# A hybrid SSM and sparse-attention model on one core: the SSM's scan in four chunks of 64 tokens instead of two of 128

## The chip, the core and the metric

The kernel runs on one core of a Trainium2 chip. Its engines work side by side, each through its own queue in order: TensorE (PE; PEld are its weight loads), VectorE (DVE), ScalarE (ACT), GpSimd (POOL) and SyncE (SP), which here only issues DMAs. The metric is the device time of one execution in microseconds. The kernel before takes 858.65 us (median of 3 runs, 856.76 to 860.2).

## The reference: what is computed

Two layers on 256 tokens of width 1024, all in float32. Each layer adds a mixer and then a gated feed-forward block of width 2816. The mixer runs a state-space branch (SSM) and an attention branch with three kinds of keys, and merges them by gates. The SSM is what the change touches:

```python
def s5_mixer(u, a_re, a_im, log_dt, b_re, b_im, c_re, c_im, d, w_glu):
    ...
    mag = jnp.exp(lr * dt)
    ab_re = mag * jnp.cos(li * dt)
    ab_im = mag * jnp.sin(li * dt)
    ...
    bu_re = jnp.einsum('bsgh,gph->bsgp', uf, b_re.astype(f32))
    ...
    _, _, x_re, x_im = lax.associative_scan(complex_affine_combine, (a_seq_re, a_seq_im, bb_re, bb_im), axis=1)
    y = (jnp.einsum('bsgp,ghp->bsgh', x_re, c_re.astype(f32))
         - jnp.einsum('bsgp,ghp->bsgh', x_im, c_im.astype(f32))
         + d.astype(f32).reshape(SSM_GROUPS, SSM_GROUP) * uf)
```

So each of 32 x 64 states follows x[t] = a x[t-1] + b[t] with one complex a of its own over the 256 tokens.

## The kernel before, in words

States lie on the 128 partitions in 16 slices a layer, which are worked on in 4 groups q of 4 slices; tokens run along the columns. A complex scan is made real by rotation: the input is multiplied by a table of cos and sin of the angle times t, scanned with the real magnitude, and turned back. The tables (E, one for cos and one for sin) hold 16 slices times TC = 128 steps; they start again in each chunk of 128 tokens, so two chunks make 256 tokens.

- `rot_powers` squares the rotation again and again: pw[i] is its power 2^i, and pw[7], times the magnitude's power, carries the state over a whole chunk. `rot_half` doubles the table in 7 steps from 1 to 128 columns, for one half (8 slices) at a time, three VectorE operations a step (two into E, one into tb). Layer 0 builds its tables at the beginning of its mixer (`p_par`, `p_tb`), layer 1's are asked for in layer 0's feed-forward.
- `ssm_a(q, h)` ("A" in ORDER) takes a group's input through small matmuls into psb, multiplies it with the tables (bc, bs, 512 columns each) and combines into z, laid out as chunk, part, slice, step. POOL writes the magnitudes into rm.
- `ssm_b2(q)` ("B") scans chunk 0: two scans (real and imaginary part) of 4 x 128 = 512 columns. Then four operations on POOL (cy three times, then z) rotate the last state of the chunk and add it to the first column of chunk 1. `ssm_c2(q)` ("C") scans chunk 1.
- `ssm_d(q, h)` ("D") multiplies z with the tables (pr) and sums over the states by matmuls into psy, then adds the direct term (yf), applies gelu and splits (y).

Other work in the same stretch: the projections' rope (`rope2`: a copy by ScalarE, four small DMAs into the one buffer tagged sw, three operations rt, sw, rt on VectorE; in layer 1 the sw product runs on POOL), the compression of keys (`c_in`: DMAs of kvc into kr, which has the same one buffer, sums kk on VectorE; `c_w1`: matmuls ps_c), the gates' matmuls ps_g, and the splits of weights into two float32r parts (wh by ScalarE, wl by VectorE). rb is the norm's scale for each token: VectorE computes it as dg, TensorE spreads it (ps_n), ScalarE copies it.

The instructions of all engines are put in order by a planner that runs a timeline of its own while the kernel is built: of what is ready on an engine in that timeline it takes what stands first in the program, which is the list ORDER. So an item may run well before or after its neighbours in ORDER, and the queues' order changes when sizes change. The pad tiles only set addresses.

Of the kernel before, what the change touches and what calls it, by code (L numbers as in the profile page):

```python
# [4 lines left out]
F32 = mybir.dt.float32  # L5
# [9 lines left out]
T = 256  # L15
KD = 8
NF = 22
NS = 16
TC = 128
NCMP = 15  # L20
CH = 1024
NEG = -1e30
# [17 lines left out]
for _name, _w in [("ropec", 256), ("ropes", 256), ("ident", 128), ("causal", 128),  # L40
# [48 lines left out]
def body(tc, ctx, d, out):  # L89
# [5 lines left out]
    raws = pool("raws", NRAW)  # L95

    pad = lambda name, n: pool(name).tile([128, n // 4], F32, name=name)
    pad("pad0", 96)
    whs = pool("whs", NWH)
    pad("pad3", 128)  # L100
    wls = pool("wls", NWL)
# [96 lines left out]
    N2 = L * NS  # L198
    par = cst.tile([128, 5, N2], F32, name="par")
    pi = cst.tile([128, N2], I32, name="pi")  # L200
    pw = cst.tile([128, 8, 3, N2], F32, name="pw")
    R, WR, WI, FR, FI = range(5)
    def tt(o, a, b, op, e=V):
        return e.tensor_tensor(o, a, b, op=op)  # L204
# [82 lines left out]
    def rot_powers():  # L287

        t = cst.tile([128, N2], F32, name="tpw")
        V.tensor_copy(pw[:, 0, 0], par[:, WR])  # L290
        ts(pw[:, 0, 1], par[:, WI], -1.0, OP.mult)
        V.tensor_copy(pw[:, 0, 2], par[:, WI])
        for i in range(7):
            stt(t, pw[:, i, 2], -2.0, pw[:, i, 2], OP.mult, OP.mult)
            stt(pw[:, i + 1, 1:3], pw[:, i, 1:3], 2.0, pw[:, i, 0:1].to_broadcast([128, 2, N2]), OP.mult, OP.mult)
            ts(pw[:, i + 1, 0], t, 1.0, OP.add)
        tt(pw[:, 7], pw[:, 7], par[:, R:R + 1].to_broadcast([128, 3, N2]), OP.mult)

    def rot_room(e):
        E = pp.tile([128, 2, NS, TC], F32, name="E", tag="E")  # L300
# [1 line left out]
        e.memset(E[:, 1, :, 0:1], 0.0)  # L302
        return E

    def rot_half(E, l, h, e, tpool, nsb=2, steps=range(7)):

        NQ = 8
        j = slice(h * NQ, (h + 1) * NQ)
        jl = slice(l * NS + h * NQ, l * NS + (h + 1) * NQ)
        tb = tpool.tile([128, 2, NQ, TC // 2], F32, name="tb", tag="sb", bufs=nsb)  # L310
        for i in steps:
            s = 1 << i
            br = pw[:, i, 0:1, jl, None].to_broadcast([128, 2, NQ, s])
# [96 lines left out]
    def mixer(l, nm, sc, first, mp, sm_):  # L410
# [132 lines left out]
        def ssm_a(q, h):  # L543

            B = sv["B"]
            Ec, Es = sv["sc"][:, 0], sv["sc"][:, 1]
            if h == 0:
                rt = mp.tile([128, 4, TC], F32, name="rm", tag="rm", bufs=1)
                G.tensor_copy(rt, par[:, R, sl0 + 4 * q:sl0 + 4 * q + 4, None].to_broadcast([128, 4, TC]))
                G.memset(rt[:, :, 0:1], 0.0)  # L550
                st[q] = mp.tile([128, 2, 2, 4, TC], F32, name="z", tag="z", bufs=NZ), rt
            z = st[q][0]
            psb = [bank("psb", "aux") for _ in range(2)]
            with row():
                for c in range(2):
                    for a in range(2):
                        r = slice(64 * h + 32 * a, 64 * h + 32 * a + 32)
                        PE.matmul(psb[a][:, c * T:(c + 1) * T], B[r, q, c, :], uy[q][r, :], start=True, stop=True,
                                  skip_group_check=True)
            bc = mp.tile([128, 2, 2, 2, TC], F32, name="bc", tag="sb", bufs=2)  # L560
            bs = mp.tile([128, 2, 2, 2, TC], F32, name="bs", tag="sb", bufs=2)
            for a in range(2):
                j = 4 * q + 2 * h + a
                src = psb[a].rearrange("p (r t) -> p r t", t=TC)
                for o, e in ((bc, Ec), (bs, Es)):
                    tt(o[:, a].rearrange("p r c t -> p (r c) t"), src,
                       e[:, j, None, :].to_broadcast([128, 4, TC]), OP.mult)
# [10 lines left out]

        def ssm_b2(q):

            z, rt = st[q]
            scan(q, 0)
            cy = sm_.tile([128, 2, 2, 4], F32, name="cy", tag="cy", bufs=2)
            zl = z[:, 0, :, :, TC - 1]
            e = eng("cy")
            tt(cy[:, 0], zl, pw[:, 7, 0:1, sl0 + 4 * q:sl0 + 4 * q + 4].to_broadcast([128, 2, 4]), OP.mult, e)
            tt(cy[:, 1], zl[:, ::-1, :], pw[:, 7, 1:3, sl0 + 4 * q:sl0 + 4 * q + 4], OP.mult, e)
            tt(cy[:, 0], cy[:, 0], cy[:, 1], OP.add, e)
            tt(z[:, 1, :, :, 0], z[:, 1, :, :, 0], cy[:, 0], OP.add, e)

        def ssm_c2(q):
            scan(q, 1)

        def ssm_d(q, h):

            z, rt = st[q]
            Ec, Es = sv["sc"][:, 0], sv["sc"][:, 1]
            Cm = sv["C"]
            if h == 0:
                sv["psy"] = bank("psy", "aux")  # L600
            psy = sv["psy"]
            for i, (c, e, ci) in list(enumerate(((0, Ec, 0), (1, Es, 1), (0, Es, 2), (1, Ec, 2))))[2 * h:2 * h + 2]:
                prs = []
                for b in range(2):
                    pr = lt.tile([128, 2, 2, TC], F32, name="pr", tag="ss", bufs=NSS)
                    j = 4 * q + 2 * b
                    tt(pr, z[:, :, c, 2 * b:2 * b + 2, :].rearrange("p k a t -> p a k t"),
                       e[:, j:j + 2, None, :].to_broadcast([128, 2, 2, TC]), OP.mult, eng("pr", 2 * i + b))
                    prs.append(pr)
                with row():  # L610
                    for a in range(4):
                        PE.matmul(psy[32 * a:32 * a + 32, :T], Cm[:, ci, 4 * q + a, :],  # L612
                                  prs[a // 2][:, a % 2].rearrange("p c t -> p (c t)"),
                                  start=(i == 0), stop=(i == 3), skip_group_check=True, tile_position=(0, 32 * a))
# [291 lines left out]
    def ffn(l, nm, mp):  # L906
# [29 lines left out]
        for m in range(KD):  # L936
# [10 lines left out]
            if l + 1 < L:  # L947
                nx.part(m)
                if m == 0:
                    tabs = rot_room(eng("t1"))  # L950
                if m < 6:
                    h = m // 3
                    rot_half(tabs, l + 1, h, eng("t1", h), mp, 1, (range(5), (5,), (6,))[m % 3])
                if m in AHEAD:
                    i = len(ahead)
                    ahead.append(split_ahead(l + 1, f"u{i}", (["th"] * 4, ["th"] * 4, ["pt"] * 4, ["ss"] * 4)[i]))
                if m % 4 == 3:
                    nc.sync.dma_start(xd[:, m - 3:m + 1, :], x[:, m - 3:m + 1, :])
            else:
                nx.square(m)  # L960
# [203 lines left out]
```

## Time and profile before

| what | value |
|---|---|
| median of 3 runs | 858.65 us |
| the profiled execution's own time | 857.34 us |
| its span, first to last instruction | 855.6 us |
| TensorE busy | 811.8 us (95%) |
| VectorE busy | 680.3 us (80%) |
| ScalarE, GpSimd busy | 415.3 us, 24.5 us |
| mean granted TensorE clock | 0.974 |

The layers follow one another: mixer and feed-forward of layer 0 up to about 435 us, those of layer 1 after that. In a list of busy time by windows each engine's busy microseconds of the window stand beside its instruction count; PEclk is the granted clock as a share of full speed. In a timeline a row has start, duration, engine, line, operation, output and inputs, shapes, count, and in brackets the idle time before it with what ended it. A row's line is often that of a helper that records the operation (L204 is every tensor_tensor), so rows are told apart by their tiles.

### The profile page before, as it was taken

The numbers are of one execution on the slowest core, as the hardware profiler recorded it, in microseconds if no ns is written. First come the engines' busy times: TensorE is split into PE (matmuls) and PEld (weight loads), VectorE is DVE, ScalarE is ACT, GpSimd is POOL, SyncE is SP. The second block draws the span as 40 slices with busy tenths as digits, with TensorE's granted clock in tenths as the row PEclk, the third lists the DMA queues.
The fourth block names the chain that finished last, engine by engine and source line by source line (L and its number), as shares of the span: only waits on it lengthen the run. The fifth ranks groups of instructions, "written<-read, shape, count | busy, mean of one in ns | idle before, by whom it ended". The sixth has DMA issues, their size and how long they took to land.

```text
span 855.6 us, 16260 instructions
## 1 busy us (share of the span) xinstructions
PE 811.8 (95%) x6420; PEld 736.9 (86%) x6420; DVE 680.3 (80%) x1284; ACT 415.3 (49%) x779; POOL 24.5 (3%) x58
## 2 busy tenths in 40 slices
PE   8997999999989999999999779999999999999994
PEld 7875786669989999999989567776899999999994
DVE  7979876747998988877767989897498888887553
ACT  3011244664544765555533136667456555665540
POOL 0000000000000000000001120100000000000000
PEclk9998999999999999999999979999999999999997
DMA  7545723515555666657744663133346566556531
GB/s 289 164 116 172 261 75 91 196 59 168 178 167 163 192 197 197 196 172 247 249 169 114 206 221 99 56 119 124 123 173 196 174 197 197 196 190 192 192 121 49
DMA packets 41772, 142.42 MB, mean 166 GB/s; under 512 B 5216, under 2 KB 6752, under 8 KB 41696
## 3 DMA queue, kind: packets, MB, share of 16 engines
q1 hardware_dynamic: 39712, 139.15, 50.3%
q10 hardware_dynamic: 1984, 2.24, 0.9%
q8 instruction: 50, 0.82, 0.4%
q14 instruction: 26, 0.21, 0.1%
HBM read 136.39 MB, written 2.10 MB: 162 GB/s over the span
## 4 chain that ended last, share of the span: by engine, by line
PE 75%; DVE 15%; DMA 5%; issue 3%; ACT 1%; POOL 0%; DVEq 0%; ACTq 0%; SPq 0%
PE ps_f L170 9%; PE ps_f L171 9%; PE ps_f L169 9%; PE ps_g L416 4%; PE ps_fo L171 4%; PE ps_fo L170 4%; PE ps_fo L169 4%; DVE z L577 2%; PE ps_g L171 2%; PE ps_g L170 2%; PE ps_g L169 2%; PE psy L612 2%; DMA raw<-wst 2%; DVE pr L204 2%; PE ps_br L169 2%
## 5 line engine op out<-in xcount | busy, mean ns | idle before, releaser
L158 ACT CAST wh<-raw 128x1024 fp32r<-128x1024 f32 (+1 forms) x199 | 207.7, 1047 | 222.7 <-PE ps_f L170 97.0
L160 DVE TENSOR_TENSOR wl<-raw,wh 128x1024 fp32r<-128x1024 f32 (+1 forms) x199 | 243.8, 1227 | 67.0 <-ACT wh L158 66.1
L170 PE MATMUL ps_f<-al,wh 128*128 128x256 f32 x704 | 195.2, 277 | 2.3 <-DVE al L213 2.3
L169 PE MATMUL ps_f<-ah,wh 128*128 128x256 f32 x704 | 195.3, 278 | 1.2 <-DVE x L213 1.2
L171 PE MATMUL ps_f<-ah,wl 128*128 128x256 f32 x704 | 194.9, 277 | 0.0
L170 PEld LDWEIGHTS ps_f<-al,wh 128*128 128x128 f32 x704 | 132.9, 189 | 2.5 <-DVE al L213 2.5
L169 PEld LDWEIGHTS ps_f<-ah,wh 128*128 128x128 f32 x704 | 132.9, 189 | 1.3 <-ACT wh L158 1.3
L171 PEld LDWEIGHTS ps_f<-ah,wl 128*128 128x128 f32 x704 | 132.8, 189 | 0.0
L171 PE MATMUL ps_fo<-fh,wl 128*128 128x256 f32 x352 | 96.9, 276 | 0.2 <-DVE wl L160 0.2
L170 PE MATMUL ps_fo<-fl,wh 128*128 128x256 f32 x352 | 97.0, 276 | 0.0
L169 PE MATMUL ps_fo<-fh,wh 128*128 128x256 f32 x352 | 96.9, 276 | 0.0
L171 PEld LDWEIGHTS ps_fo<-fh,wl 128*128 128x128 f32 x352 | 65.9, 188 | 0.4 <-DVE wl L160 0.4
L170 PEld LDWEIGHTS ps_fo<-fl,wh 128*128 128x128 f32 x352 | 66.1, 188 | 0.0
L169 PEld LDWEIGHTS ps_fo<-fh,wh 128*128 128x128 f32 x352 | 66.1, 188 | 0.0
L416 PE MATMUL ps_g<-xg,raw 128*128 128x256 f32 x256 | 63.9, 399 | 1.0 <-ACT hs L664 0.4
L416 PEld LDWEIGHTS ps_g<-xg,raw 128*128 128x128 f32 x256 | 48.9, 199 | 12.0 <-issue 4.9
L204 DVE TENSOR_TENSOR pr<-z,E 128x512 f32<-128x512 f32 x64 | 43.2, 720 | 8.7 <-PE psy L612 8.7
L169 PE MATMUL ps_g<-ah,wh 128*128 128x256 f32 x128 | 40.6, 317 | 6.3 <-ACT wh L158 4.7
L213 DVE SCALAR_TENSOR_TENSOR cv<-ab,sp,cv 128x255 f32<-128x255 f32 (+1 forms) x88 | 42.0, 480 | 1.7 <-ACT cv L917 0.4
L171 PE MATMUL ps_g<-ah,wl 128*128 128x256 f32 x128 | 40.1, 313 | 2.8 <-DVE wl L160 2.7
L170 PE MATMUL ps_g<-al,wh 128*128 128x256 f32 x128 | 40.0, 313 | 0.0
L577 DVE TENSOR_TENSOR_SCAN z<-rm,z 128x512 f32<-128x512 f32 x32 | 37.7, 1209 | 2.3 <-POOL z L204 2.3
(259 smaller groups left out, 1671.6 us busy)
## 6 DMA issues: line engine op xcount, KB each, us to landing
raw<-wst SPq DMA_DIRECT2D x246, 512.0 KB, 4.2
x<-xT SPq DMA_DIRECT2D x4, 512.0 KB, 4.9
raw<-wst SPq DMA_DIRECT2D x4, 420.0 KB, 3.5
B<-wst SPq DMA_DIRECT2D x2, 512.0 KB, 6.2
xd<-x SPq DMA_DIRECT2D x2, 512.0 KB, 6.5
x<-xd SPq DMA_DIRECT2D x2, 512.0 KB, 6.1
sw<-rt SPq DMA_DIRECT2D x12, 64.0 KB, 3.4
sw<-rt ACTq DMA_DIRECT2D x12, 64.0 KB, 3.8
```

The costliest lines, as they stand in the source:

```text
L158: S.copy(h[:, :n], t[:, :n])
L160: V.tensor_tensor(lo[:, :n], t[:, :n], h.bitcast(F32)[:, :n], op=OP.subtract)
L169: PE.matmul(ps, wh, ah, start=start, stop=False, **k)
L170: PE.matmul(ps, wh, al, start=False, stop=False, **k)
L171: PE.matmul(ps, wl, ah, start=False, stop=stop, **k)
L204: return e.tensor_tensor(o, a, b, op=op)
L213: e.scalar_tensor_tensor(o, a, s, b, op0=op0, op1=op1)
L416: PE.matmul(ps, w[:, k * 128:(k + 1) * 128], xg[:, k, :], start=k == 0, stop=k == KD - 1, skip_group_check=True)
L577: V.tensor_tensor_scan(f, rt.rearrange("p a t -> p (a t)"), f, 0.0, op0=OP.mult, op1=OP.add)
L612: PE.matmul(psy[32 * a:32 * a + 32, :T], Cm[:, ci, 4 * q + a, :], prs[a // 2][:, a % 2].rearrange("p c t -> p (c t)"), start=(i == 0), sto ...
```

## The change

TC goes from 128 to 64, so the sequence has NK = 4 chunks. Tables have 64 columns a slice and 6 doubling steps (LV = 6) instead of 7. A group is scanned in 4 pairs of 4 x 64 = 256 columns, with a carry after each but the last. "B" scans chunk 0, and "C" has a chunk number now and comes three times, spread in ORDER over the stretch where it stood once. Products with the tables cover the same columns in runs of 64. One pad grows by 128 bytes.

```diff
-TC = 128
+TC = 64
+NK = T // TC
+LV = 6
...
-     'cw:0:2 cw:0:3 g:2:0 mc B:1 C:0 ck D:0:0 D:0:1 ...
+    ('par tb:0 q:1 kc mb q:0 pf cin tb:1 A:0:0 A:0:1 ks v B:0 xn A:1:0 A:1:1 g:0:0 g:0:1 C:0:1 sa g:1:0 cw:0:0 '
+     'cw:0:1 cw:0:2 C:0:2 cw:0:3 g:2:0 mc B:1 C:0:3 ck D:0:0 D:0:1 ...
-    pad("pad0", 96)
+    pad("pad0", 224)
...
-    pw = cst.tile([128, 8, 3, N2], F32, name="pw")
+    pw = cst.tile([128, LV + 1, 3, N2], F32, name="pw")
...
-        for i in range(7):
+        for i in range(LV):
...
-    def rot_half(E, l, h, e, tpool, nsb=2, steps=range(7)):
+    def rot_half(E, l, h, e, tpool, nsb=2, steps=range(LV)):
...
-                st[q] = mp.tile([128, 2, 2, 4, TC], F32, name="z", tag="z", bufs=NZ), rt
+                st[q] = mp.tile([128, NK, 2, 4, TC], F32, name="z", tag="z", bufs=NZ), rt
...
         def ssm_b2(q):
 
+            ssm_k(q, 0)
+
+        def ssm_k(q, k):
+
             z, rt = st[q]
-            scan(q, 0)
+            scan(q, k)
+            if k == NK - 1:
+                return
             cy = sm_.tile([128, 2, 2, 4], F32, name="cy", tag="cy", bufs=2)
-            zl = z[:, 0, :, :, TC - 1]
+            zl = z[:, k, :, :, TC - 1]
...
-            tt(z[:, 1, :, :, 0], z[:, 1, :, :, 0], cy[:, 0], OP.add, e)
-
-        def ssm_c2(q):
-            scan(q, 1)
+            tt(z[:, k + 1, :, :, 0], z[:, k + 1, :, :, 0], cy[:, 0], OP.add, e)
+
+        def ssm_c2(q, k):
+            ssm_k(q, k)
...
-                    rot_half(tabs, l + 1, h, eng("t1", h), mp, 1, (range(5), (5,), (6,))[m % 3])
+                    rot_half(tabs, l + 1, h, eng("t1", h), mp, 1, (range(4), (4,), (5,))[m % 3])
```

## Rows read from the trace of the kernel before

**Rows 1.** Busy time by engine: us, share of the span, instructions.

```profile
PE 811.8 (95%) x6420; PEld 736.9 (86%) x6420; DVE 680.3 (80%) x1284; ACT 415.3 (49%) x779; POOL 24.5 (3%) x58
```

**Rows 2.** Windows: length, then busy us of PE, PEld, DVE, ACT, POOL; clock, DMA.

```profile
40.00:60.00 20.00, 20.00 (x102) 16.19 (x101) 16.45 (x28) 1.69 (x3) 0.00 (x0) 1.00 0.37 109
...
60.00:80.00 20.00, 13.36 (x64) 10.16 (x63) 19.12 (x30) 3.89 (x7) 2.23 (x6) 0.83 0.49 155
...
68.00:72.00 4.00, 2.86 (x12) 1.74 (x13) 4.00 (x7) 1.74 (x2) 0.00 (x0) 0.50 0.32 57
...
240.00:260.00 20.00, 16.48 (x128) 16.11 (x127) 19.24 (x40) 8.04 (x14) 0.00 (x0) 0.91 0.44 134
...
300.00:320.00 20.00, 20.00 (x178) 20.00 (x178) 17.84 (x29) 12.09 (x20) 0.00 (x0) 1.00 0.66 202
...
480.00:500.00 20.00, 16.73 (x151) 11.61 (x151) 17.69 (x29) 4.32 (x10) 0.78 (x4) 0.83 0.62 201
```

**Rows 3.** What TensorE waited for in 56–126 us: total us, times, longest.

```profile
PE ps_c L660 <- DVE kk L204: 6.2, 1, 6.2
```

**Rows 4.** What TensorE waited for in 180–262 us: total us, times, longest.

```profile
PE ps_f L170 <- DVE al L213: 2.3, 1, 2.3
PE ps_f L169 <- DVE x L213: 1.2, 1, 1.2
```

**Rows 5.** Groups of VectorE by form: busy us, mean ns, idle before with releaser.

```profile
L577 DVE TENSOR_TENSOR_SCAN z<-rm,z 128x512 f32<-128x512 f32 x32 | 37.7, 1209 | 2.3 <-POOL z L204 2.3
...
L204 DVE TENSOR_TENSOR E<-E,pw 128x1024 f32<-128x1024 f32 x4 | 4.9, 1222 | 0.0
...
L204 DVE TENSOR_TENSOR E<-E,pw 128x512 f32<-128x512 f32 x4 | 2.8, 688 | 0.1
```

**Rows 6.** Timeline of VectorE from the tables to kk.

```profile
27.43 1.22 DVE L204 TENSOR_TENSOR E<-E,pw 128x1024 f32<-128x1024 f32 x1
...
28.56 1.22 DVE L204 TENSOR_TENSOR tb<-E,pw 128x1024 f32<-128x1024 f32 x1
...
32.16 0.47 DVE L208 TENSOR_SCALAR dg<-cc,nt 128x128 f32<-128x128 f32 x2
...
43.24 0.69 DVE L204 TENSOR_TENSOR rt<-rt,sw 128x512 f32<-128x512 f32 x1
...
68.25 0.74 DVE L204 TENSOR_TENSOR kk<-kr,sp 128x256 f32<-128x256 f32 x2
```

**Rows 7.** Timeline of TensorE: the matmuls that spread rb.

```profile
36.92 0.61 PE L404 MATMUL ps_n<-dg,ones 128*128 128x128 f32 x4
```

**Rows 8.** Timeline of ScalarE's queue: DMAs of the ropes and of kr.

```profile
44.64 0.51 ACTq L493 DMA_DIRECT2D sw<-kvc  x1
...
60.75 1.28 ACTq L644 DMA_DIRECT2D kr<-kvc  x2
```

**Rows 9.** Timeline of VectorE: last operation on half 0 of layer 1's tables.

```profile
247.52 1.22 DVE L204 TENSOR_TENSOR E<-E,tb 128x1024 f32<-128x1024 f32 x1
```

**Rows 10.** Timeline of VectorE: scans before and after a carry.

```profile
61.39 2.34 DVE L577 TENSOR_TENSOR_SCAN z<-rm,z 128x512 f32<-128x512 f32 x2 [0.67 <-POOL z L204]
...
79.88 2.33 DVE L577 TENSOR_TENSOR_SCAN z<-rm,z 128x512 f32<-128x512 f32 x2
...
83.26 2.34 DVE L577 TENSOR_TENSOR_SCAN z<-rm,z 128x512 f32<-128x512 f32 x2 [1.05 <-POOL z L204]
...
114.28 1.23 DVE L577 TENSOR_TENSOR_SCAN z<-rm,z 128x512 f32<-128x512 f32 x1 [0.17 <-POOL z L204]
...
469.48 2.33 DVE L577 TENSOR_TENSOR_SCAN z<-rm,z 128x512 f32<-128x512 f32 x2
...
474.68 2.34 DVE L577 TENSOR_TENSOR_SCAN z<-rm,z 128x512 f32<-128x512 f32 x2 [0.38 <-POOL z L204]
```

**Rows 11.** Timeline of POOL: two carries' first operations, one rope product.

```profile
82.29 0.36 POOL L204 TENSOR_TENSOR cy<-z,pw 128x8 f32<-128x8 f32 x2 [17.35 <-DVE z L577]
...
471.89 1.52 POOL L204 TENSOR_TENSOR cy<-z,pw 128x8 f32<-128x8 f32 x2 [5.22 <-DVE z L577]
...
511.55 1.73 POOL L204 TENSOR_TENSOR sw<-sw,rc 128x512 f32<-128x512 f32 x1 [8.50 <-DMA sw<-rt]
```

More of the change, by code (lines that the diff above doesn't have):

```diff
@@ L296, in rot_powers @@
             ts(pw[:, i + 1, 0], t, 1.0, OP.add)
-        tt(pw[:, 7], pw[:, 7], par[:, R:R + 1].to_broadcast([128, 3, N2]), OP.mult)
+        tt(pw[:, LV], pw[:, LV], par[:, R:R + 1].to_broadcast([128, 3, N2]), OP.mult)
     def rot_room(e):
@@ L559, in ssm_a @@
                                   skip_group_check=True)
-            bc = mp.tile([128, 2, 2, 2, TC], F32, name="bc", tag="sb", bufs=2)
-            bs = mp.tile([128, 2, 2, 2, TC], F32, name="bs", tag="sb", bufs=2)
+            bc = mp.tile([128, 2, 2, NK, TC], F32, name="bc", tag="sb", bufs=2)
+            bs = mp.tile([128, 2, 2, NK, TC], F32, name="bs", tag="sb", bufs=2)
             for a in range(2):
@@ L566, in ssm_a @@
                     tt(o[:, a].rearrange("p r c t -> p (r c) t"), src,
-                       e[:, j, None, :].to_broadcast([128, 4, TC]), OP.mult)
+                       e[:, j, None, :].to_broadcast([128, 2 * NK, TC]), OP.mult)
             for c, op in ((0, OP.add), (1, OP.subtract)):
@@ L579, in ssm_b2 @@
         def ssm_b2(q):
+            ssm_k(q, 0)
+        def ssm_k(q, k):
             z, rt = st[q]
-            scan(q, 0)
+            scan(q, k)
+            if k == NK - 1:
+                return
             cy = sm_.tile([128, 2, 2, 4], F32, name="cy", tag="cy", bufs=2)
-            zl = z[:, 0, :, :, TC - 1]
+            zl = z[:, k, :, :, TC - 1]
             e = eng("cy")
-            tt(cy[:, 0], zl, pw[:, 7, 0:1, sl0 + 4 * q:sl0 + 4 * q + 4].to_broadcast([128, 2, 4]), OP.mult, e)
-            tt(cy[:, 1], zl[:, ::-1, :], pw[:, 7, 1:3, sl0 + 4 * q:sl0 + 4 * q + 4], OP.mult, e)
+            tt(cy[:, 0], zl, pw[:, LV, 0:1, sl0 + 4 * q:sl0 + 4 * q + 4].to_broadcast([128, 2, 4]), OP.mult, e)
+            tt(cy[:, 1], zl[:, ::-1, :], pw[:, LV, 1:3, sl0 + 4 * q:sl0 + 4 * q + 4], OP.mult, e)
             tt(cy[:, 0], cy[:, 0], cy[:, 1], OP.add, e)
-            tt(z[:, 1, :, :, 0], z[:, 1, :, :, 0], cy[:, 0], OP.add, e)
-        def ssm_c2(q):
-            scan(q, 1)
+            tt(z[:, k + 1, :, :, 0], z[:, k + 1, :, :, 0], cy[:, 0], OP.add, e)
+        def ssm_c2(q, k):
+            ssm_k(q, k)
         def ssm_d(q, h):
@@ L604, in ssm_d @@
                 for b in range(2):
-                    pr = lt.tile([128, 2, 2, TC], F32, name="pr", tag="ss", bufs=NSS)
+                    pr = lt.tile([128, 2, NK, TC], F32, name="pr", tag="ss", bufs=NSS)
                     j = 4 * q + 2 * b
                     tt(pr, z[:, :, c, 2 * b:2 * b + 2, :].rearrange("p k a t -> p a k t"),
-                       e[:, j:j + 2, None, :].to_broadcast([128, 2, 2, TC]), OP.mult, eng("pr", 2 * i + b))
+                       e[:, j:j + 2, None, :].to_broadcast([128, 2, NK, TC]), OP.mult, eng("pr", 2 * i + b))
                     prs.append(pr)
```

19 rows, old and new, of the table ORDER are left out of this document.

## The prediction

> **What bounds the kernel now.** I read the busy shares first, then the busy time by windows of 20 us, then the waits and the timeline of the stretches that were not full. TensorE is busy 811.8 of 855.6 us [rows 1], and in the feed-forward halves a window like 300–320 us is full [rows 2]. So a change of VectorE's work can pay only where TensorE stands still. The reader is to see three such places. In 60–80 us TensorE is busy 13.36 of 20 us while VectorE is busy 19.12; in 240–260 us it is 16.48 against 19.24; in 480–500 us it is 16.73 against 17.69 [rows 2]. After the first of these the granted clock is 0.50 in 68–72 us, the lower level of 1.2 GHz, right behind a stretch in which TensorE had nothing [rows 2]. The first idle is one wait: the compression matmul ps_c waits 6.2 us for VectorE's kk [rows 3]. The second is ps_f waiting for al and x, 2.3 and 1.2 us [rows 4]. The third stands in layer 1's mixer, where VectorE carries the SSM and the weight splits together.
>
> **a. Layer 0's tables.** The last doubling step has three operations of 128x1024 for each half of a table; in four half tables that is 12 operations, 4 of each of three names, of which one is shown [rows 5]. All 12 go; the steps that stay keep their sizes. They cost 1.13 us from start to start (27.43 to 28.56 [rows 6]). In layer 0 six of them lie ahead of the rope's operation at 43.24 [rows 6]: 6 x 1.13 = 6.8 us. The step of powers that goes with them is three operations on at most 64 columns, under 0.5 us, and I leave it out. TensorE is full there, so nothing is gained at once. What counts is how kk gets earlier. Its chain runs: rotary tables scaled by rb, which needs dg (32.16 [rows 6]) and then TensorE's ps_n (36.92 [rows 7]); the rope of the first q, whose last operation at 43.24 [rows 6] frees the one sw tile; then the DMA of kvc at 44.64, a second use of sw, the DMA into kr at 60.75 [rows 8]; and kk at 68.25 [rows 6]. Three of the six operations stand ahead of dg, so dg could come 3.4 us earlier. If ps_n keeps its place behind the ps_kc group, the rope still sheds the 1024-column operations between rb and 43.24, some 1.6 us (my estimate: one whole operation of 1.13 and the part of another). If ps_n moves ahead of that group, the chain moves by nearly the whole 6.8. Against it stand group 0's share of the new costs below, which are also ahead of kk. The most to be had is the idle of 6.2 us plus the lower clock behind it: 2.86 us of matmuls ran at the lower level [rows 2], about 1.4 us lost, together 7.6. The least is 0. I take 5.5, close to the 6.2 that the wait shows, because VectorE is almost full in 60–80 us, and work that it has finished earlier is then out of kk's way even where the DMAs set the pace.
>
> **b. Layer 1's tables.** They are not built where the code calls for them, in the second half of the feed-forward, but in gaps that the planner saw around the second idle; the last operation of half 0 is at 247.52 [rows 9], ahead of the al and x that TensorE waits for at about 250 us. Three of the six operations, 3.4 us, go from ahead of that wait. But the planner fills what it takes for gaps: half 1's smaller steps, which now come behind it, can move up and take the same time. So: at most 3.5 of idle [rows 4] and 1.8 of clock (0.91 in that window [rows 2]: 18% of 20 us at the lower level, half of it lost), 5.3 gained; at worst 1.0 lost to refilled gaps; I take 1.0 gained. The other three operations lie in the feed-forward proper, which hides them: TensorE is full there.
>
> **c. More, shorter scans.** Each group of four slices had 4 scans of 512 columns and gets 8 of 256, so 32 become 64 [rows 5]. Per column the cost is the same; what is added is the fixed part. For an elementwise operation it is 2 x 688 - 1222 = 154 ns by durations [rows 5]; two scans back to back take 2.34 us (61.39 [rows 10]), which is 1.13 each against a duration of 1.209 [rows 5], so about 0.08 of the fixed part overlaps with the neighbour. 0.07 us is left for each added scan: 4 x 0.07 = 0.28 us a group. The bounds are 0 and 4 x 0.154 = 0.62. Exposed are group 0 of layer 0 (ahead of kk) and three groups of layer 1: 4 x 0.28 = 1.1 us (0 to 2.5). The others lie beside matmuls of the gates. The products and sums of 512 columns, read in runs of 64 instead of 128, cost the same: a table step of 512 columns that is made of short runs takes 688 ns [rows 5], the duration of the other products of that size.
>
> **d. More carries.** A group had one carry, four small operations on POOL between two scans, and gets three in series: 16 more. From the end of a scan pair to the next scan a carry takes 1.05 us where VectorE has nothing else (79.88 + 2.33 to 83.26 [rows 10]) and 2.87 us beside other work (469.48 + 2.33 to 474.68 [rows 10]). Queued behind the waiting scan on VectorE are the group's later products and all splits and ropes that the planner put behind it, and for these TensorE waits. What VectorE lost is less, since other work stood in between: 0.67, 1.05 and 0.17 us in layer 0's first three groups and 0.38 us in layer 1, 2.3 in all [rows 10], the sum in the scans' row [rows 5]. Counting two further carries at what the group's present one lost: layer 0's group 0, 2 x 0.67 = 1.3 us; its later groups cost nothing, as gate matmuls are there to run; layer 1, two groups in its stretch of idle, 4 x 0.38 = 1.5 us. I take 2.8. The bounds are 0 (all filled) and 12 x 1.05 = 12.6 (six groups, nothing filled).
> One rule speaks against this edit. The four cy operations are tiny, but the pair took 0.36 us at 82.29, where VectorE stood still, and 1.52 us at 471.89 beside VectorE's splits [rows 11]. The Trainium skill ("SBUF — State Buffer", section "SBUF: two separate sides") says why: VectorE with two SBUF inputs and GpSimd hold one port pair in turn, each for a whole instruction. By that rule, each added carry in a full stretch is the 2.87 us one rather than the 1.05 us one, and more of it would be exposed than I count; what it would do here is part of the second rival.
>
> **Sum.** -5.5 - 1.0 + 1.1 + 2.8 = -2.6 us. The profiled execution took 857.34 us, 1.3 below the median of 858.65 of the runs shown; 858.65 - 2.6 gives 856.0.
>
> **Rivals.**
> 1. *The whole idle goes.* ps_n moves up, kk comes before TensorE needs it, no clock falls there, and the gap at 250 us closes too: -7.6 - 5.3 + 1.1 = -11.8, 846.9 us. For it: both waits name VectorE [rows 3, 4]. Against it: two DMA round trips stay in kk's chain, and half 1's steps wait to fill the gap.
> 2. *POOL becomes the wait, and it is slower.* In layer 1 POOL also multiplies the ropes' sw, in order: at 511.55 it had stood 8.50 us for that DMA [rows 11]. A carry put behind such an instruction holds the next scan for as long, and VectorE with it. With one carry per group none fell there; with three it is likelier. Price: one such stay of 8.5, and three further carries at 2.87 instead of 1.05, 5.5; with c 1.1, less a and b, 6.5: +8.6, 867 us. It decides as soon as layer 1's scans lose more than 6.5 us to POOL.
> 3. *The freed time was spare.* kk hangs on its DMAs, ps_n stays, the gap at 250 us is refilled: a is 1.0, b 0, c and d half exposed at 2.0: +1.0, 859.7 us. For it: TensorE is full in 40–60 us [rows 2], and the six operations lie ahead of that.
> That the tables were not shortened, or the scans not split, is excluded by the code: sizes follow TC.
>
> **Chances.** Forecast 0.45 (own range 852 to 860), rival 1 0.15, rival 2 0.21, rival 3 0.19. About 0.5% (4.3 us, from 854.4 to 862.9) is what a measurement of this kernel can tell from no change. Faster takes all of rival 1 and 0.22 of the forecast's 0.45, as re-planned queues move things by a few us either way: 0.37. Slower takes rival 2 and a little of rival 3: 0.23. Same: 0.40. The range, 847 to 866, reaches from rival 1 to nearly rival 2.
>
> **What would show it.** Right: no table operation of 1024 columns; 64 scans of about 0.68 us; POOL's cy, cy sum and z operations three times as many; ps_c's wait for kk near 1 us; 60–80 us with TensorE busy 18 or more; VectorE's wait for POOL's z some 5 us in all instead of 2.3. Wrong: a wait for kk still above 4 us (step a, then rival 3); TensorE idle in 470–545 us grown by more than 4 us with POOL's sw or cy named (step d, then rival 2); VectorE's busy time down by less than 8 us of the 13.6 that go.

## The result and the profile after

The changed kernel takes 864.68 us (median of 4 runs) where the kernel before took 858.74 beside it: ratio 1.0077, 95% interval 1.0048 to 1.0105. It is slower by 6 us; the forecast was 856.0. The profiled execution took 865.77 us, 8.43 more than the one of before; so the stages below, which come from this one pair of profiles, add up to 2.5 us more than the medians differ by.

Where the time went is seen when the span is cut at the last matmul of each stage: the end of layer 0's mixer (last ps_wo), of its feed-forward (last ps_fo), of layer 1's mixer and of its feed-forward. First the kernel before, cut so (bounds, length, then busy us of PE, PEld, DVE, ACT, POOL, the clock, DMA share, GB/s):

```profile
0.00:244.71 244.71, 232.77 (x1510) 188.89 (x1510) 195.04 (x476) 98.14 (x231) 7.09 (x28) 0.97 0.50 162
244.71:432.72 188.01, 184.26 (x1605) 183.90 (x1606) 159.91 (x258) 106.17 (x161) 0.00 (x0) 0.99 0.64 201
432.72:660.81 228.09, 211.73 (x1701) 181.51 (x1701) 183.80 (x323) 114.07 (x246) 15.83 (x28) 0.96 0.43 141
660.81:841.73 180.92, 180.92 (x1599) 180.92 (x1598) 135.06 (x206) 96.14 (x142) 0.00 (x0) 1.00 0.54 175
```

The kernel after, the same cut:

```profile
0.00:250.11 250.11, 239.43 (x1512) 194.45 (x1513) 189.04 (x486) 102.14 (x235) 14.64 (x60) 0.95 0.50 159
250.11:433.18 183.07, 182.33 (x1605) 182.06 (x1605) 153.56 (x249) 105.43 (x159) 0.00 (x0) 1.00 0.68 206
433.18:669.18 236.00, 218.82 (x1701) 188.74 (x1701) 183.15 (x339) 117.14 (x248) 25.85 (x60) 0.93 0.43 136
669.18:850.10 180.92, 180.92 (x1599) 180.92 (x1598) 135.05 (x206) 96.25 (x142) 0.00 (x0) 1.00 0.54 175
```

Layer 0's mixer costs 5.40 us more, its feed-forward 4.94 less, layer 1's mixer 7.91 more, its feed-forward the same: 8.37 of the 8.43. TensorE's idle time in layer 1's mixer is 17.2 us (236.00 - 218.82) where it was 16.4, and in layer 0's it is 10.7 where it was 11.9. The rest of both losses is TensorE "busy" at a lower clock (0.95 for 0.97 in layer 0, 0.93 for 0.96 in layer 1): not more waiting in all, but the same matmuls at the lower level for longer.

The rows that answer to those of before. Busy time by engine [rows 1]:

```profile
PE 823.7 (95%) x6420; PEld 747.9 (87%) x6420; DVE 667.2 (77%) x1301; ACT 421.7 (49%) x783; POOL 42.1 (5%) x122
```

VectorE shed 13.1 us and TensorE is "busy" 11.9 us longer with the same 6420 matmuls. Windows [rows 2]:

```profile
60.00:80.00 20.00, 15.34 (x70) 11.94 (x69) 18.90 (x30) 3.33 (x5) 2.78 (x12) 0.83 0.48 145
68.00:72.00 4.00, 4.00 (x12) 3.22 (x11) 4.00 (x7) 1.05 (x1) 0.00 (x0) 0.55 0.10 41
240.00:260.00 20.00, 19.26 (x167) 19.02 (x167) 19.46 (x44) 11.04 (x18) 0.00 (x0) 1.00 0.53 161
...
480.00:500.00 20.00, 17.47 (x166) 13.05 (x165) 18.64 (x32) 4.92 (x11) 1.19 (x4) 0.88 0.71 211
500.00:520.00 20.00, 17.40 (x103) 16.61 (x102) 17.25 (x27) 7.34 (x10) 9.50 (x16) 0.66 0.65 219
```

The last of these before:

```profile
500.00:520.00 20.00, 15.59 (x109) 13.28 (x108) 17.86 (x28) 8.20 (x13) 4.43 (x4) 0.83 0.63 213
```

The idle at 250 us is gone, the one in 60–80 us only smaller, and in 500–520 us the clock is 0.66 for 0.83. What TensorE waited for in 56–126 us [rows 3]:

```profile
PE ps_g L418 <- issue: 4.7, 1, 4.7
PE ps_g L418 <- DMA raw<-wst: 1.5, 2, 0.9
```

The wait for kk is gone and a wait of 4.7 us in front of the gates' ps_g has its place. VectorE by form [rows 5], then POOL by form, first after and then before:

```profile
L579 DVE TENSOR_TENSOR_SCAN z<-rm,z 128x256 f32<-128x256 f32 x64 | 41.0, 677 | 10.7 <-POOL z L206 10.5
...
L206 DVE TENSOR_TENSOR E<-E,pw 128x512 f32<-128x512 f32 x4 | 2.8, 688 | 0.1
```

```profile
L206 POOL TENSOR_TENSOR cy<-z,pw 128x8 f32<-128x8 f32 x48 | 14.6, 327 | 211.0 <-DVE z L579 173.7 <-DVE mx L210 33.0 <-DVE kr L650 1.5
```

```profile
L204 POOL TENSOR_TENSOR cy<-z,pw 128x8 f32<-128x8 f32 x16 | 5.4, 359 | 200.2 <-DVE z L577 200.2
```

No step of 1024 columns, 64 scans of 0.68 us, three times the carries, and VectorE waits 10.5 us for POOL's z where it waited 2.3.

### The profile page after: what moved, and what is told of

Its sections match the earlier page's. It is cut to its first block, busy times and chain, and to the rows that moved or that the text cites. A ratio compares the mean times of both kernels' runs of the same rounds, so it can differ in the third digit from the quotient of the medians.

```text
span 863.9 us, 16348 instructions
## 1 busy us (share of the span) xinstructions
PE 823.7 (95%) x6420; PEld 747.9 (87%) x6420; DVE 667.2 (77%) x1301; ACT 421.7 (49%) x783; POOL 42.1 (5%) x122
## 4 chain that ended last, share of the span: by engine, by line
PE 81%; DVE 7%; issue 5%; DMA 3%; ACT 2%; POOL 1%; DVEq 0%; ACTq 0%; SPq 0%; POOLq 0%
PE ps_f L171 9%; PE ps_f L172 9%; PE ps_f L173 9%; PE ps_g L418 7%; PE ps_fo L172 5%; PE ps_fo L173 5%; PE ps_fo L171 5%; PE psy L620 2%; PE ps_br L171 2%; PE ps_br L173 2%; PE ps_br L172 2%; PE ps_s L755 2%; PE ps_q L418 2%; PE ps_g L171 2%; PE ps_g L173 2%
## 5 line engine op out<-in xcount | busy, mean ns | idle before, releaser
L418 PE MATMUL ps_g<-xg,raw 128*128 128x256 f32 x256 | 65.7, 408 | 6.2 <-issue 4.7
L579 DVE TENSOR_TENSOR_SCAN z<-rm,z 128x256 f32<-128x256 f32 x64 | 41.0, 677 | 10.7 <-POOL z L206 10.5
```

Of the source, the lines that this page charges most:

```text
L418: PE.matmul(ps, w[:, k * 128:(k + 1) * 128], xg[:, k, :], start=k == 0, stop=k == KD - 1, skip_group_check=True)
L579: V.tensor_tensor_scan(f, rt.rearrange("p a t -> p (a t)"), f, 0.0, op0=OP.mult, op1=OP.add)
```

## The experiments

Theory 1: the added carries and scans cost the time, as a chain in layer 1's mixer. Theory 2: every change of sizes makes the planner deal the queues anew, and the order that the kernel before has in layer 1's mixer is an unusually good one. Theory 3, formed later: POOL's carries have a price of their own beside that. To speak of order, I compared the sequences of matmuls in TensorE's queues: "moved" is the number of the 1515 queue entries of layer 1's mixer that lie outside the common sequence with the kernel before. The count goes by long equal runs and is not the smallest possible, so it is a rough measure; the argument rests on the places where it is 0 between two kernels. Each kernel was timed against the kernel before in five rounds; stage lengths are from its one profile, cut as above. Layer 1's feed-forward took 180.92 us in all of them.

| kernel | us | ratio to before, 95% | mixer 0 | feed-fwd 0 | mixer 1 | moved |
|---|---|---|---|---|---|---|
| before (profile) | | | 244.7 | 188.0 | 228.1 | 0 |
| after (profile) | 864.7 | 1.0077, 1.0048–1.0105 | 250.1 | 183.1 | 236.0 | 382 |
| tables | 857.5 | 0.9993, 0.9977–1.0008 | 242.7 | 183.1 | 235.6 | 195 |
| chunks | 863.7 | 1.0072, 1.0044–1.0099 | 244.1 | 187.6 | 236.5 | 382 |
| scan2 | 863.8 | 1.0073, 1.0045–1.0101 | 244.6 | 187.5 | 236.5 | 443 |
| nocarry | 862.7 | 1.0060, 1.0041–1.0079 | 244.4 | 183.0 | 237.1 | 199 |
| swap409 | 864.4 | 1.0082, 1.0057–1.0108 | 245.2 | 187.5 | 234.1 | 409 |
| swap133 | 861.1 | 1.0033, 1.0009–1.0056 | 247.2 | 186.6 | 231.9 | 133 |
| late | 854.6 | 0.9955, 0.9939–0.9972 | 247.3 | 182.0 | 229.7 | 66 |
| late0 | 857.1 | 0.9987, 0.9969–1.0006 | 243.1 | 183.3 | 235.4 | 195 |
| after_order | 870.3 | 1.0124, 1.0092–1.0156 | 248.4 | 183.5 | 237.7 | 186 |
| after_sw1 | 863.1 | 1.0052, 1.0037–1.0067 | 249.1 | 183.3 | 233.2 | 225 |
| after_sw2 | 868.6 | 1.0109, 1.0081–1.0137 | 248.4 | 182.9 | 239.7 | 373 |
| after_m1 | 867.4 | 1.0092, 1.0068–1.0117 | 249.6 | 183.4 | 238.4 | 382 |
| after_m3 | 862.0 | 1.0031, 1.0010–1.0053 | 252.1 | 183.1 | 233.2 | 394 |
| cyv | 856.9 | 0.9977, 0.9953–1.0002 | 244.1 | 182.8 | 234.7 | 233 |
| cyv_order | 854.7 | 0.9962, 0.9944–0.9980 | 244.7 | 182.8 | 230.8 | 155 |
| cyv_sw1 | 860.6 | 1.0018, 0.9997–1.0039 | 244.2 | 182.9 | 235.4 | 434 |
| cyv_sw2 | 860.9 | 1.0034, 1.0017–1.0051 | 244.1 | 182.9 | 236.1 | 371 |
| cyv_m3 | 858.8 | 0.9992, 0.9974–1.0010 | 244.9 | 183.1 | 234.1 | 344 |

Of before, swap409, swap133, late and late0, TensorE's queue in layer 0's mixer is the same, and it took 243.1 to 247.3 us; of after, chunks and after_m1 it is the same in layer 1's mixer, which took 236.0 to 238.4. That much, 4.2 and 2.4 us, one profile of a stage can differ by, and the 228.1 us of before are one profile too.

### One part at a time: tables, chunks, scan2

tables (kernel before; E and tb built with TE = 64; it leaves out the rotation of each chunk's second half):

```diff
-                       e[:, j, None, :].to_broadcast([128, 4, TC]), OP.mult)
+                       e[:, j // 2, None, :].to_broadcast([128, 4, TC]), OP.mult)
...
-            rot_half(tabs, l + 1, h, eng("t1", h), mp, 1, (range(5), (5,), (6,))[m % 3])
+            rot_half(tabs, l + 1, h, eng("t1", h), mp, 1, (range(4), (4,), (5,))[m % 3])
```

> The kernel before with tables of 64 steps alone: two chunks of 128 and one carry a group stay, and each product over 128 columns reads the 64-step tables of two slices side by side (the second half's own rotation is left out). It has steps a and b of the prediction without c and d. Theory 1 (the three carries in series and the shorter scans cost the time in layer 1's mixer): the tables' gain shows whole, 853 to 856 us, and layer 1's attention and gates end as far behind the feed-forward as in the kernel before. Theory 2 (any change of sizes makes the planner re-order the queues, and the new order of TensorE's matmuls is thinner and runs at a lower clock): no gain is sure; 858 to 866 us, the granted clock below 0.974, with some of the 8 us of layer 1's mixer lost here too.

857.5 us, ratio 0.9993. The feed-forward gained its 4.9 us, and layer 1's mixer, whose scans and carries are those of the kernel before, gave back 7.5:

```profile
242.73:425.87 183.14, 182.39 (x1605) 181.98 (x1605) 153.48 (x249) 104.85 (x159) 0.00 (x0) 1.00 0.67 206
425.87:661.50 235.63, 217.38 (x1701) 185.07 (x1701) 183.26 (x323) 114.75 (x246) 17.28 (x28) 0.94 0.43 137
```

Theory 1 has no place for this loss. The time lies between the two ranges: theory 2 holds for layer 1's mixer, and the gain before it was larger than I had put it there.

chunks (kernel after, the seventh doubling step kept):

```diff
-        E = pp.tile([128, 2, NS, TC], F32, name="E", tag="E")
+        E = pp.tile([128, 2, NS, 2 * TC], F32, name="E", tag="E")
...
-    def rot_half(E, l, h, e, tpool, nsb=2, steps=range(LV)):
+    def rot_half(E, l, h, e, tpool, nsb=2, steps=range(7)):
```

> The kernel after with the seventh doubling step still built (128-step tables, of which the first 64 steps are read): steps c and d without a and b. Theory 1: before plus the whole cost of scans and carries, 867 to 871 us (the kernel after, 864.7, plus the 3 to 6 us that its shorter tables gave at the end of layer 0's feed-forward). Theory 2: the order is dealt anew, so anything from 859 to 870 us, with no tie to the sum.

863.7 us, below theory 1's range and within theory 2's. The feed-forward's gain is absent (187.6), layer 1's mixer lost its 8.4 us, and layer 0's mixer, with all carries on POOL, lost nothing.

scan2 (kernel before, each scan issued as two):

```diff
-            f = z[:, k, c].rearrange("p a t -> p (a t)")
-            V.tensor_tensor_scan(f, rt.rearrange("p a t -> p (a t)"), f, 0.0, op0=OP.mult, op1=OP.add)
+            for b in range(0, 4, 2):
+                    f = z[:, k, c, b:b + 2].rearrange("p a t -> p (a t)")
+                    V.tensor_tensor_scan(f, rt[:, b:b + 2].rearrange("p a t -> p (a t)"), f, 0.0, op0=OP.mult,
+                                         op1=OP.add)
```

> The kernel before with each scan of 512 columns issued as two of 256: 32 more VectorE instructions, the same columns, no more carries and the same tables. It is step c alone, 1.1 us of VectorE by the forecast. Theory 1: 858 to 860 us. Theory 2: 443 of layer 1's 1515 matmuls move; its mixer takes 234 to 238 us and the kernel 864 to 868.

863.8 us, within 0.2 us of theory 2's range and four beyond theory 1's. Sixteen added instructions of 0.1 us each in a mixer (step c below) cannot make 8.4 us by their own length.

### The order alone: swap409, swap133

Two neighbours of layer 1's ORDER in the kernel before exchange places; no operation changes (of ORDER only the part that differs is shown, here and below).

```diff
-v C:0 cw:0:2 D:0:0 cw:1:0 cw:0:3
+v C:0 cw:0:2 cw:1:0 D:0:0 cw:0:3
```

> The kernel before with two neighbours in layer 1's ORDER exchanged (cw:1:0 ahead of D:0:0). No operation is added, removed or resized; the planner deals layer 1's mixer anew, and 409 of TensorE's 1515 matmuls in it stand at another place in its queue (382 in the kernel after, 195 with short tables alone). Theory 1 (the carries and scans cost the time): 858 us, as before, because nothing of them changes. Theory 2 (the order that the kernel before has in layer 1's mixer is an unusually good one, and any other costs about 7 to 8 us there): 864 to 867 us, layer 1's mixer 235 to 237 us instead of 228.

864.4 us, ratio 1.0082: a loss as large as the changed kernel's, without any of its work. Layer 1's mixer is 6.0 us longer, a little less than theory 2's 7 to 8:

```profile
432.67:666.77 234.10, 212.10 (x1701) 181.07 (x1701) 183.36 (x323) 116.86 (x248) 18.94 (x28) 0.96 0.42 137
```

The clock is 0.96 as before, and the loss stands as idle time: 22.0 us for 16.4. Most of it is in one place. TensorE in 585–595 us, before and then with the exchange:

```profile
585.00:595.00 10.00, 10.00 (x72) 5.86 (x71) 6.71 (x12) 6.67 (x13) 0.00 (x0) 1.00 0.27 94
```

```profile
585.00:595.00 10.00, 6.18 (x41) 5.15 (x40) 6.16 (x13) 8.90 (x27) 0.00 (x0) 0.87 0.44 148
```

And what TensorE does there with the exchange, in the timeline (start, duration; in brackets the idle time before it):

```profile
586.06 0.28 PE L171 MATMUL ps_g<-ah,wl 128*128 128x256 f32 x1
...
588.84 0.38 PE L169 MATMUL ps_glu<-y,wh 128*128 128x256 f32 x1 [1.48 <-DVE th L204]
...
592.15 0.89 PE L783 MATMUL ps_o<-pT,vt 128*64 128x256 f32 x4 [2.34 <-ACT pT L780]
```

The gates' last ps_g is at 586.06; in the kernel before, ps_g is there to run until 597.2. With the fill work spent early, the last group's chain and the attention's end stand alone there.

swap133 exchanges g:1:1 and g:2:0:

> The kernel before with two other neighbours in layer 1's ORDER exchanged (g:2:0 ahead of g:1:1): again the same operations; 133 of 1515 matmuls at another place. Theory 1: 858 us. Theory 2: layer 1's mixer some us longer, 860 to 866 us in all; if the loss goes by how many matmuls move, about 861.

861.1 us, ratio 1.0033, layer 1's mixer 3.8 us longer: theory 2 again, with its size about by the count. The count is not a law, though: 155 to 443 moved gave anything from 2.7 to 11.6 us.

### The tables' gain without the change: late, late0

```diff
-                    rot_half(tabs, l + 1, h, eng("t1", h), mp, 1, (range(5), (5,), (6,))[m % 3])
+                    with tc.issue_after(posts[LATE].ins):
+                        rot_half(tabs, l + 1, h, eng("t1", h), mp, 1, (range(5), (5,), (6,))[m % 3])
```

posts[i] is the feed-forward's last product of slice i; LATE is 2 in late and 0 in late0. The SSM is that of the kernel before.

> The kernel before with layer 1's tables (still of 128 steps) held back until the third slice of layer 0's feed-forward is done, so that none of their operations stands ahead of the al and x for which TensorE waits at about 250 us. This is the gain of step b without any change of the SSM: layer 0's feed-forward 183 us instead of 188. Theory 1: nothing else changes, 853 to 854 us. Theory 2: layer 1's mixer is dealt anew (66 of its 1515 matmuls move), so part of the 5 us is given back there: 854 to 860 us.

> The same kernel as late, with layer 1's tables held back until the first slice of layer 0's feed-forward is done, not the third. The work is that of the kernel before; TensorE's queue in layer 1's mixer is now, matmul for matmul, the one of the kernel with short tables alone (195 of 1515 away from the kernel before), where late has 66. Layer 0's feed-forward should gain some 5 to 6 us as in late (182 to 183 us). Theory 1: 854 to 855 us, as late. Theory 2: layer 1's mixer takes 234 to 236 us as with short tables, not 229.7, and the kernel 858 to 861 us.

late takes 854.6 us, ratio 0.9955 (0.9939–0.9972), and is faster than both kernels. Its feed-forward has no idle time left, and layer 1's mixer lost 1.6, less than two profiles of one queue differ by:

```profile
247.31:429.31 182.00, 182.00 (x1605) 181.87 (x1605) 159.80 (x272) 105.71 (x158) 0.00 (x0) 1.00 0.67 206
429.31:658.99 229.68, 212.76 (x1701) 182.31 (x1701) 183.57 (x323) 114.45 (x246) 16.52 (x28) 0.96 0.43 140
```

The time, 854.6, is 0.6 above theory 1's range and within theory 2's, and does not decide between them. late0 differs by where the same 42 table operations may begin. TensorE's queue in layer 1's mixer is then matmul for matmul that of tables, VectorE's has the same sequence too, and so is the time, 235.39 for 235.63:

```profile
426.45:661.84 235.39, 217.34 (x1701) 185.11 (x1701) 183.21 (x323) 114.53 (x246) 17.43 (x28) 0.94 0.43 137
```

So what layer 1's mixer lost with short tables was its order. In all 20 profiles the stage ends 58.4 to 61.8 us behind the last psy, though it lasts from 228.1 to 239.7: what an order costs arises ahead of the SSM's last sums, and shows in how late they come. In all late0 took 857.1 us, 2.6 above late and one below theory 2's range. In its profile layer 0's mixer, of the same queue, was 4.2 us shorter than late's (243.14 for 247.31); that fits, but it is one profile against one.

### The carries: cyv, nocarry, and eight other orders

cyv is the kernel after with the carry on VectorE; nocarry is the kernel after without any carry, so each chunk starts from zero (of the line that names the engines, the one entry is shown):

```diff
-cy="G"
+cy="V"
```

```diff
             scan(q, k)
-            if k == NK - 1:
-                return
+            return
```

> The kernel after with its carry's four operations on VectorE instead of POOL: no hop between two engines, nothing of POOL's rope product in between, but 96 more small VectorE operations. Theory 1: most of the chain's waits (z behind POOL 10.5 us in the kernel after) go, 858 to 861 us. Theory 2: the order is dealt anew and VectorE gets some 6 us more work; 861 to 868 us, with the clock still about 0.962.

> The kernel after with all carries left out (each chunk starts from zero): scans of 256 columns stay, nothing chains them. Theory 1: the whole cost of d goes and the kernel is faster than before by about the tables' gain, 853 to 856 us, clock back at 0.974. Theory 2: 859 to 866 us, a clock well below 0.974, and layer 1's attention and gates still late.

cyv took 856.9 us, as theory 1 has it (a little below its range). But nocarry, with nothing in the chain at all, took 862.7, as theory 2 has it: its layer 1 mixer was no shorter than the changed kernel's (237.1 for 236.0). (The lower clock that theory 2 named did not come: 0.974 over the whole span.) As the whole account theory 1 falls with that; since nocarry has an order of its own, it doesn't show how much of the changed kernel's loss is carries. Why cyv is fast was still to be settled, and the remaining kernels draw other orders for either place of the carry.

after_order and cyv_order move items of layer 1's ORDER, with the sequence inside the SSM, inside attention and inside each gate kept (after_order's first and last lines; cyv_order's are of the same kind):

```diff
-sa mb A:0:0 kc q:1 cin A:0:1 cw:0:0 A:1:0 q:0 B:0 cw:0:1 C:0:1 ks A:1:1 C:0:2 v C:0:3 cw:0:2 D:0:0 cw:1:0
+sa mb A:0:0 kc q:1 cin A:0:1 cw:0:0 A:1:0 q:0 cw:0:1 B:0 C:0:1 A:1:1 ks v cw:0:2 cw:1:0 C:0:2 C:0:3 D:0:0 B:1
...
-C:3:2 g:0:1 C:3:3 g:3:0 g:2:1 D:3:0 g:6:0 gs:3:1 av:1:1 g:6:1 D:3:1
+D:3:0 g:3:0 g:0:1 gs:3:1 g:2:1 D:3:1 g:6:0 g:6:1
```

> The kernel after with the items of layer 1's ORDER moved against one another (SSM, gates and attention each keep their own sequence), chosen so that TensorE's queue in layer 1's mixer comes nearer to the one of the kernel before: 186 of 1515 matmuls away instead of 382. Carries, scans and tables are those of the kernel after. Theory 1: 864 to 865 us, because the chain is the same. Theory 2: the loss is one of the order; 186 is still as far as the kernel with short tables, so layer 1's mixer may keep most of its 8 us: 859 to 865 us.

> The kernel after with its carry on VectorE and layer 1's ORDER moved in the same way (155 of 1515 away from the kernel before instead of 233). Theory 1: 857 us as with the carry on VectorE alone. Theory 2: 851 to 858 us, layer 1's mixer 229 to 235 us instead of 234.7; a candidate for a version that beats both kernels.

after_order became slower still, 870.3 us, outside both ranges: nearness in count to the queue of before helps nothing by itself. cyv_order took 854.7 us, ratio 0.9962 (0.9944–0.9980), which also beats both kernels. The pairs sw1 and sw2 are the exchanges of swap409 and swap133 in layer 1's ORDER; m1 and m3 are in layer 0's:

```diff
-gs:1:1 A:3:0 as:0:1:0 C:2:2
+gs:1:1 as:0:1:0 A:3:0 C:2:2
...
-cw:0:3 g:2:0 mc B:1
+cw:0:3 mc g:2:0 B:1
```

> The kernel after with cw:1:0 ahead of D:0:0 in layer 1's ORDER: no work is changed, 263 of 1515 matmuls of layer 1's mixer stand elsewhere than in the kernel after. If POOL's carries have a price of their own (theory 3), the kernel stays in the band of its two relatives, 862 to 870 us, above the one with the carry on VectorE under the same exchange. If the order alone decides (theory 2), 855 to 870 us with no tie to the carry's place.

> The kernel after with the carry on VectorE and the same exchange (cw:1:0 ahead of D:0:0). Theory 3: 853 to 859 us, 5 us or more below after_sw1. Theory 2: 855 to 866 us, on either side of after_sw1.

> The kernel after with g:2:0 ahead of g:1:1 in layer 1's ORDER: 315 of 1515 matmuls stand elsewhere. Theory 3: 862 to 870 us. Theory 2: 855 to 870 us.

> The kernel after with the carry on VectorE and g:2:0 ahead of g:1:1. Theory 3: 853 to 859 us, 5 us or more below after_sw2. Theory 2: 855 to 866 us, on either side of after_sw2.

> The kernel after with as:0:1:0 ahead of A:3:0 in layer 0's ORDER: 44 of layer 0's 1088 matmuls in the mixer move, layer 1's queue on TensorE stays as it is. If the order alone makes the 5 us in layer 0's mixer (theory 2), it comes out anywhere from 243 to 250 us, and layer 1's at 236; 858 to 865 us. If POOL's carries make them (theory 3), layer 0's mixer stays at 248 to 250 us; 863 to 866 us.

> The kernel after with mc ahead of g:2:0 in layer 0's ORDER: 171 of 1088 matmuls move in layer 0's mixer and 110 of 1515 in layer 1's. Theory 2: layer 0's mixer 243 to 250 us. Theory 3: 248 to 250 us, above cyv_m3 by 4 us or more.

> The same exchange (mc ahead of g:2:0 in layer 0's ORDER) in the kernel after with the carry on VectorE: 60 of 1088 and 212 of 1515 matmuls move. Theory 2: layer 0's mixer 243 to 250 us. Theory 3: 243 to 245 us.

Six orders with the carry on POOL took 862.0 to 870.3 us (mean 866.0), five with it on VectorE 854.7 to 860.9 (mean 858.4); under the same ORDER, POOL's is above by 7.8 (as given), 2.6 (sw1), 7.8 (sw2) and 3.3 us (m3), 5.4 on average. That is theory 3 by its direction. By its numbers it was missed in places: sw1 gave less than the 5 us asked for, cyv_sw1, cyv_sw2 and after_m1 came out 1.4 to 1.9 us above its ranges, after_m3's layer 0 mixer 2.1 above its own, and each place of the carry spans 6 to 8 us by order alone. As moving the carry deals the queues anew as well, these numbers don't part POOL's price from the order's. By stages the profiles differ by 5.2 us in layer 0's mixer (248.4 to 252.1 against 244.1 to 244.9, in three and two orders there) and by 2.2 in layer 1's (means 236.4 and 234.2), which is no more than one queue's profiles differ by.

How POOL's carry makes 5 us in layer 0 isn't settled. Its own length in the last group is free. VectorE there, carry on POOL (scans, then the group's first products, then its sum):

```profile
153.29 1.27 DVE L579 TENSOR_TENSOR_SCAN z<-rm,z 128x256 f32<-128x256 f32 x2 [1.04 <-POOL z L206]
156.51 1.27 DVE L579 TENSOR_TENSOR_SCAN z<-rm,z 128x256 f32<-128x256 f32 x2 [0.83 <-POOL z L206]
...
173.93 0.69 DVE L206 TENSOR_TENSOR pr<-z,E 128x512 f32<-128x512 f32 x1
...
187.88 0.48 DVE L215 SCALAR_TENSOR_TENSOR yf<-u,sp,psy 128x256 f32<-128x256 f32 x1 [0.86 <-PE psy L620]
```

The same with the carry on VectorE:

```profile
154.91 0.24 DVE L206 TENSOR_TENSOR cy<-z,pw 128x8 f32<-128x8 f32 x2
...
155.60 1.27 DVE L579 TENSOR_TENSOR_SCAN z<-rm,z 128x256 f32<-128x256 f32 x2
...
172.74 1.29 DVE L206 TENSOR_TENSOR pr<-z,E 128x512 f32<-128x512 f32 x2
...
183.20 0.48 DVE L215 SCALAR_TENSOR_TENSOR yf<-u,sp,psy 128x256 f32<-128x256 f32 x1 [1.67 <-PE psy L620]
```

The last scans end 0.9 us apart (157.8 and 156.9), some 16 us before anything reads them, the group's first products (by count the 25th of the layer's 32) start 1.2 us apart, and yet the last yf is 4.7 us apart: 3.5 of it arises behind the first products, where products, psy, attention and glu alternate in another order. But TensorE was behind before that, and not for want of work. Up to 170 us and in 100–125 us, first after, then cyv:

```profile
0.00:170.00 170.00, 162.08 (x900) 127.34 (x901) 131.27 (x372) 57.56 (x152) 14.64 (x60) 0.94 0.52 166
100.00:125.00 25.00, 25.00 (x148) 21.32 (x146) 21.34 (x56) 12.12 (x34) 2.90 (x14) 0.73 0.32 99
```

```profile
0.00:170.00 170.00, 161.91 (x909) 126.31 (x910) 136.55 (x419) 57.48 (x151) 2.82 (x12) 0.95 0.52 168
100.00:125.00 25.00, 25.00 (x154) 20.71 (x153) 22.51 (x68) 13.77 (x39) 0.50 (x2) 0.80 0.29 88
```

With the carry on POOL it is busy for as long and has run 900 matmuls for 909, with a clock of 0.73 for 0.80 in 100–125 us. Another order of the same items, at another clock, is what differs; that points to the order. Against it, three orders of layer 0 with POOL's carry were all slow; against POOL, chunks has the same carries and 244.1 us. Which of the two decides there stays open.

## Why the prediction was wrong

The forecast had the direction wrong. The time lies inside its range and close to the second rival's 867, but that is luck: what made it is no term of the sum, and the rival's own condition, layer 1's scans losing more than 6.5 us to POOL, was not met (4.1).

**The step that failed is the sum itself.** It priced each part against the order of before, and allowed for re-planning only as "a few us either way". It isn't either way: in all 19 changed kernels layer 1's mixer was longer than the 228.1 us of before, by 1.6 to 11.6 us, also in the kernels whose work is unchanged (swap409 6.0, swap133 3.8, late0 7.3). The smallest, late's 1.6, is within what one queue's profiles differ by, and cyv_order's 2.7 is hardly above it. This term, left out, is worth more than the -2.6 us of the four that were in. The whole account: b -4.9, layer 1's mixer +7.9 (as much as the order alone cost elsewhere; how much of it is POOL's carries is not shown), layer 0's mixer +5.4 (present with short tables and POOL's carries together; cause open). Over all profiles of the same two queues, layer 0's mixer is 3.5 us longer (249.0 in four, 245.5 in five). The forecast's cover in step d, that layer 0's later groups "cost nothing, as gate matmuls are there to run", hangs on the order as well: in swap409's layer 1 they had run out.

**a, -5.5.** kk did come earlier, ahead of what TensorE does next, as the more favourable case had it, but not to any use. VectorE, and then TensorE in the kernel after (before: [rows 6]):

```profile
59.98 0.77 DVE L206 TENSOR_TENSOR kk<-kr,sp 128x256 f32<-128x256 f32 x2 [0.69 <-DMA kr<-kvc]
...
65.62 1.21 DVE L206 TENSOR_TENSOR xg<-xg,rb 128x1024 f32<-128x1024 f32 x1
...
67.96 1.21 DVE L206 TENSOR_TENSOR xg<-xg,rb 128x1024 f32<-128x1024 f32 x1
```

```profile
66.94 6.01 PE L418 MATMUL ps_g<-xg,raw 128*128 128x256 f32 x16 [4.66 <-issue]
72.88 0.67 PE L668 MATMUL ps_c<-raw,kk 128*32 128x256 f32 x8
```

kk starts 8.3 us earlier than at 68.25. But the planner had put ps_g ahead of ps_c, and ps_g reads xg after its product with rb: the first half of that ends at 66.83 (65.62 + 1.21), and ps_g starts at 66.94. The profile names nothing for the 4.66 us; by these times the wait for kk, 6.2, became a wait for xg. With the tables alone layer 0's mixer gained 2.0 us, within what profiles of one order differ by; nothing of a is shown.

**b, -1.0** (bound -5.3). It was -4.9 in the profile after and -4.5 to -5.2 in every kernel with short tables: both waits of [rows 4] are gone, and the window 240–260 us runs at 1.00 for 0.91. The gaps weren't refilled to any harm. late shows the same with long tables, so it is the place of the operations ahead of al and x that counts, and the term should have been near its bound.

**c, +1.1.** Two scans back to back take 1.27 us where two of double length took 2.33, so an added scan costs 0.10 us of VectorE and not 0.07; VectorE's scans took 3.3 us more in all. What of it lies on the path can't be read off: scan2's 6 us are re-dealt order.

**d, +2.8.** VectorE's wait for POOL's z is 10.5 us, not some 5: it grew by 8.2 where d had 2.8. Most of it, 6.3, stands in layer 0, and 4.1 in layer 1, where rival 2 wanted more than 6.5 (433–669 us):

```profile
L579 DVE TENSOR_TENSOR_SCAN z<-rm,z 128x256 f32<-128x256 f32 x32 | 20.5, 678 | 4.3 <-POOL z L206 4.1
```

What of it reached the time isn't shown: TensorE's waits don't name it, and the 5.4 and 7.7 us between POOL and VectorE above have the order in them. Nor is 12.6 a bound, as it takes 1.05 us for each carry and the prediction's own slow one took 2.87. Rival 2's place for it, a carry held 8.5 us behind a rope product, did not come. A product did cut in between, for 1.28 us (POOL in layer 1):

```profile
499.81 0.91 POOL L206 TENSOR_TENSOR cy<-z,pw 128x8 f32<-128x8 f32 x2 [17.38 <-DVE z L579]
500.68 1.28 POOL L206 TENSOR_TENSOR sw<-sw,rc 128x512 f32<-128x512 f32 x1
501.92 0.20 POOL L206 TENSOR_TENSOR cy<-cy 128x8 f32<-128x8 f32 x1
```

The port rule of the Trainium skill ("SBUF — State Buffer", section "SBUF: two separate sides") (the two engines hold one port pair in turn) agrees in kind: such a pair takes 0.91 us here, beside VectorE's rope product (0.67 us from 499.65), and took 0.36 where VectorE stood [rows 11]. But the longer pairs don't make those 7.7 us: the mean of an operation of this form is 327 ns over all carries, and was 359 before.

**The signs named ahead.** VectorE's busy time fell by 13.1 us and POOL's operations tripled, as forecast; 60–80 us has TensorE busy 15.34, not 18. The sign for rival 2, idle grown by over 4 us in 470–545 us, did not come. Before, then after:

```profile
470.00:545.00 75.00, 64.38 (x509) 50.55 (x508) 69.78 (x118) 30.62 (x74) 11.56 (x20) 0.91 0.48 159
```

```profile
470.00:545.00 75.00, 65.70 (x486) 53.99 (x486) 65.55 (x120) 30.29 (x66) 16.79 (x37) 0.84 0.50 159
```

Idle fell from 10.6 to 9.3 us, yet 23 fewer matmuls ran: the loss there appears as the lower clock, so idle alone was the wrong thing to watch.

## What to carry to other kernels

Where a planner deals the queues from a list that was set for the old sizes, price a change in two parts: its own operations, and the loss of the order. Measure the second first, by exchanging two neighbours that change no work; here it was +3.5 and +6.8 us, where the whole change cost 6. And take a gain by the smallest edit that yields it: holding back 42 operations (late) gave the feed-forward's 6 us with 66 matmuls moved, and the kernel 0.45%.

## What was not expected of the hardware

- The same loss takes two forms. In swap409 it is 5.6 us more TensorE idle time at a clock of 0.96; in the kernel after it is 0.8 us more idle and 0.93. In swap409 the clock fell to 0.87 in 585–595 us, with two waits of 1.48 and 2.34 us in that stretch.
- A carry of four operations of 8 columns holds VectorE for 1.05 us by way of POOL ([rows 10]; 1.04 in the last group above) and takes 0.69 us on VectorE itself (154.91 to 155.60 us in cyv).
